# Residual and norm between the stages of a decoder layer: square sums chained on VectorE, weight casts queued behind the scaled rows, rounded rows written k-tile by k-tile

## The chip, the cores and the metric

One core of a Trainium2 chip runs the whole layer in one launch. The metric is device time in microseconds (us) of one execution; the number that counts is the median over several executions.

## The reference

One decoder layer, batch 1, 256 tokens, width 1024, in float32. Each of three sub-layers is normalised, modulated by a shift and a scale that come from a conditioning vector c, and added back under a gate:

```python
mod = (silu(c) @ w_ada + b_ada)                    # 9 vectors of 1024
sh1, sc1, gt1, sh2, sc2, gt2, sh3, sc3, gt3 = split(mod, 9)
n = rmsnorm(h, g_ffn1) * (1 + sc1) + sh1
h = h + 0.5 * gt1 * swiglu(n, w1_gate, w1_up, w1_down)      # d_ff = 2816
n = rmsnorm(h, g_mix) * (1 + sc2) + sh2
h = h + gt2 * hybrid_mixer(n, w_in, w_pool, pool_scale, w_out)
n = rmsnorm(h, g_ffn2) * (1 + sc3) + sh3
h = h + 0.5 * gt3 * swiglu(n, w2_gate, w2_up, w2_down)
return rmsnorm(h, g_final)
```

`rmsnorm(x, g)` is `x * rsqrt(mean(x*x) + 1e-6) * g`. The mixer projects n by `w_in` into four chunks of 512 columns (pool input u, then q, k, v), pools u over trailing windows, lets 8 heads attend over three dilated windows, and projects both by `w_out`.

## The kernel before

**Numbers.** Every large product is made of three matmuls. A float32 operand is split into a rounded part (`hi` for weights, `nh` for rows) and what is left (`lo`, `nl`); the matmuls are nh by hi, nl by hi and nh by lo, added up in PSUM (`gemm`, L344; `down`, L379; `lead_step`, L404). So each weight unit (128 x 2048 floats, 1 MB) that has landed in one of four `raw` buffers is cast twice per half: `hi` on ScalarE (L241) and `lo` on VectorE (L242), into one of 11 half-unit buffers each. The tokens are two tiles of 128 rows, t = 0 and t = 1.

**Order of the weights.** `plan()` writes out by hand the order of 114 units; SyncE's queue loads them in that order (L225) as `raw` buffers come free. Between the weight units stand 36 units called `ada`: two rows of `w_ada` per unit, multiplied by silu(c) and summed on VectorE (L230, two instructions for each unit), which gives two columns of `mod`. `want()` fetches so far ahead that five weight units lie behind the one in use. Around the first of the two norms that this change touches the order is: down 7, 8, 9, 10 of the first feed-forward with the last `ada` units that its norm needs; then `win` (1,0), ada, `win` (1,1), ada, `win` (2,0), ada, `win` (2,1), ada, `win` (3,0), ada, `win` (3,1). `win` (c, half) is half of the 1024 input rows of the projection's chunk c (1 is q, 2 is k, 3 is v, 0 is u). When `finish1(0)` is written, everything up to `win` (3,0) has been fetched, four `ada` units of the mixer's gate among it.

**Order on an engine.** The instructions of each engine are put in a fixed order when the program is built: a list schedule by priority, in which an instruction whose inputs are ready goes ahead of a more urgent one whose inputs are not. `urgent()` raises the priority of what stands on the path between stages, `ADA` lowers that of the `ada` products. On the chip each engine then runs its list in that order.

**First norm of the change (feed-forward 1 to mixer).** At the end of `ffn_rest` the held chunks 7 to 10 are multiplied for t = 0; `finish1(0)` adds the gated result to h (`residual`: one product and one sum for each 512 columns, VectorE), sums squares on ScalarE (`rstd`, L269), adds and raises to the power -0.5 on GpSimd (L271, L273, L275), and scales the rows on ScalarE (`norm_rows`, L294). Meanwhile TensorE multiplies the same four chunks for t = 1 (48 matmuls, L386). `after()` stands before chunk number `TURN` of them: it transposes the scaled rows of t = 0 (eight transposes, `turn`, L282), then `norm_mod` applies scale and shift and splits the result into nh and nl: columns 0 to 511 are scaled on ScalarE (L311), columns 512 to 1023 on VectorE (L313), each half is split by one cast and one subtraction of 512 columns (`split`, L260 and L261). Then `zchunk` (L345 to L347) runs q for t = 0 (q0, 24 matmuls), and k0. `finish1(1)` does the same for t = 1; its transposes stand inside k0, before k-tile 1. q1 follows, then k1, v0 and the rest.

**Second norm of the change (mixer to feed-forward 2).** `wout` runs t = 0, then t = 1 (48 matmuls, L675); `finish2(0)`'s transposes stand before its last chunk (`TURN1` = 3). The first four k-tiles of the second feed-forward (`lead_step`, L416) run for t = 0 alone; `finish2(1)`'s transposes stand before the last of them (`TURN2` = 3). Here columns 512 to 1023 are only copied (`xT3`, L304).

`rstd`, `norm_rows`, `norm_mod`, `residual`, `finish1`, `finish2`, `fetch` and the constants `TURN` and the new `AFTER1` are what the diff touches. Temporaries of 512 columns share three buffers (`t2`).

Of the kernel before, what the change touches and what calls it, by code (L numbers as in the profile page):

```python
# [15 lines left out]
P = 128  # L16
# [16 lines left out]
TURN = 2  # L33
TURN1 = 3
TURN2 = 3
T2 = 3
# [132 lines left out]
def block_kernel(ctx, tc, w, vec, x, c, gf, wpool, bandd, biasd, out):  # L169
# [46 lines left out]
    ready = {}  # L216
    done_mod = set()
    place = {u: i for i, u in enumerate(order)}

    def fetch():  # L220
# [5 lines left out]
        if kind == "ada":  # L226
            with tc.high_priority(offset=ADA if i >= 2 * KD else 0):
                for s, m in enumerate(a):
                    r = raw[:, ts(s, D)]
                    nc.vector.tensor_tensor_reduce(  # L230
                        r, r, cb, 1.0, vecs[:, m:m + 1], ALU.mult, ALU.add, mod[:, m:m + 1])
                    done_mod.add(m)
            return
        his, los = [], []
        for s in range(2):
# [3 lines left out]
            for o in range(0, 1024, n):  # L239
                src = raw[:, s * 1024 + o:s * 1024 + o + n]  # L240
                nc.scalar.copy(hi[:, o:o + n], src)  # L241
                nc.vector.tensor_tensor(lo[:, o:o + n], src, hi[:, o:o + n].bitcast(F32), ALU.subtract)  # L242
# [21 lines left out]
    def rstd(t, tag):  # L264

        ss = tiny.tile([P, 2], F32, name=f"ss{tag}", tag="ss")
        for b in range(2):
            sq = work.tile([P, 512], F32, name=f"sq{tag}{b}", tag="t2", bufs=T2)
            nc.scalar.activation(sq, h[:, t * D + b * 512:t * D + b * 512 + 512], AF.Square, accum_out=ss[:, b:b + 1])  # L269
            if b == 0:  # L270
                nc.gpsimd.tensor_tensor(ss[:, 0:1], ss[:, 0:1], deps, ALU.add)  # L271
        v = tiny.tile([P, 1], F32, name=f"v{tag}", tag="v")
        nc.gpsimd.tensor_tensor(v, ss[:, 0:1], ss[:, 1:2], ALU.add)  # L273
        r = tiny.tile([P, 1], F32, name=f"r{tag}", tag="r")
        nc.gpsimd.tensor_tensor(r, v, mhalf, ALU.pow)  # L275
        return r

# [11 lines left out]
    def norm_rows(t, tag):  # L289
        r = rstd(t, tag)  # L290
        xs = []
        for b in range(2):
            xs.append(work.tile([P, 512], F32, name=f"xs{tag}{b}", tag="t2", bufs=T2))
            nc.scalar.activation(xs[b], h[:, t * D + b * 512:t * D + b * 512 + 512], AF.Copy, scale=r)  # L294
        return xs

    def norm_mod(xs, which, shm, tag, t=None, xT=None):

        nh, nl = new_n(tag)
        for b in range(2):  # L300
            pt = turn(xs[b], f"xt{tag}{b}")
            with urgent():
# [4 lines left out]
                for i in range(4):  # L307
                    j = 4 * b + i
                    a, s = acol[:, which * KD + j:which * KD + j + 1], mod[:, shm * KD + j:shm * KD + j + 1]
                    if b == 0:  # L310
                        nc.scalar.activation(n32[:, i, :], pt[:, i, :], AF.Identity, bias=s, scale=a)  # L311
                    else:
                        nc.vector.tensor_scalar(n32[:, i, :], pt[:, i, :], a, s, ALU.mult, ALU.add)  # L313
# [464 lines left out]
```

## Time and profile before

| what | value |
|---|---|
| median of 3 runs | 495.44 us (495.12 to 497.16) |
| the profiled execution | 498.72 us, of which its span from the first to the last instruction is 496.7 us |
| busy: TensorE, VectorE, ScalarE, GpSimd | 476.4 us (96%), 355.3 us (72%), 257.6 us (52%), 17.2 us (3%) |
| mean granted TensorE clock | 0.995 |

Busy times are from one profiled execution; the span is what the trace covers. A share of 96% for TensorE says that it has little idle time, not where that lies.

### The profile page before, as it was taken

How to read it: one execution, taken by the hardware profiler on the slowest of the kernel's cores; microseconds unless marked ns; L12 is line 12 of the kernel's file. 1: busy time of each engine (PE TensorE's matmuls, PEld its weight loads, DVE VectorE, ACT ScalarE, POOL GpSimd, SP SyncE). 2: the span in 40 equal slices, each digit the busy share in tenths (PEclk: the TensorE clock that was granted, in tenths of full speed). 3: DMA queues.
4: the chain of work that ended last, by engine and by line, in shares of the span. 5: the costliest groups of instructions: out<-in, count | busy, mean ns of one | idle time of the engine just before them, and what ended most of it. 6: DMA issues, size and time to landing. Idle time of an engine off the chain costs nothing.

```text
span 496.7 us, 5926 instructions
## 1 busy us (share of the span) xinstructions
PE 476.4 (96%) x2151; PEld 383.6 (77%) x2151; DVE 355.3 (72%) x568; ACT 257.6 (52%) x435; POOL 17.2 (3%) x26
## 2 busy tenths in 40 slices
PE   4899999999999999899999999999999999999994
PEld 2688888888888888678766877888878888888883
DVE  5887979997797897698868767555656656655244
ACT  2667575453355453574777458945543443544121
POOL 1000000000000001120000022000000000000000
PEclk9999999999999999899999999999999999999999
DMA  8999975899988897769865847395266758540102
GB/s 318 354 336 356 346 292 201 326 364 406 338 323 330 332 328 273 266 244 379 349 226 193 284 155 281 102 367 177 105 242 252 277 221 329 185 164 2 42 2 84
DMA packets 20095, 126.05 MB, mean 254 GB/s; under 512 B 2377, under 2 KB 4193, under 8 KB 5474
## 3 DMA queue, kind: packets, MB, share of 16 engines
q1 hardware_dynamic: 17280, 121.25, 65.0%
q10 hardware_dynamic: 2786, 4.43, 2.7%
q8 instruction: 17, 0.28, 0.2%
q14 instruction: 12, 0.10, 0.0%
HBM read 124.61 MB, written 1.06 MB: 253 GB/s over the span
## 4 chain that ended last, share of the span: by engine, by line
PE 86%; ACT 3%; DVE 2%; DMA 2%; issue 2%; POOL 2%; POOLq 0%; ACTq 0%; DVEq 0%
PE accf L386 21%; PE ld L416 9%; PE le L416 9%; PE gu L345 9%; PE gu L347 9%; PE gu L346 9%; PE zp L345 3%; PE zp L347 3%; PE zp L346 3%; PE ht L372 2%; PE accm L675 1%; DMA gfb<-in_gf_dram 1%; ACT hi L241 1%; DMA vecs<-in_vec_dram 1%; PE sh L345 1%
## 5 line engine op out<-in xcount | busy, mean ns | idle before, releaser
L242 DVE TENSOR_TENSOR lo<-raw,hi 128x1024 fp32r<-128x1024 f32 (+1 forms) x160 | 186.8, 1195 | 49.7 <-ACT hi L241 41.3
L241 ACT CAST hi<-raw 128x1024 fp32r<-128x1024 f32 (+1 forms) x160 | 160.3, 1031 | 78.3 <-PE accf L386 24.9
L230 DVE CUSTOM_DVE_ANT_0 raw<-raw,cb,vecs 128x1024 f32<-128x1024 f32 x72 | 90.5, 1279 | 6.6 <-DMA raw<-in_w_dram 6.6
L386 PE MATMUL accf<-hi,hh 128*128 128x512 f32 x176 | 56.2, 395 | 0.2
L386 PE MATMUL accf<-lo,hh 128*128 128x512 f32 x176 | 56.3, 394 | 0.0
L386 PE MATMUL accf<-hi,hl 128*128 128x512 f32 x176 | 55.7, 390 | 0.0
L345 PE MATMUL gu<-hi,nhc 128*128 128x512 f32 x112 | 44.4, 397 | 0.0
L347 PE MATMUL gu<-lo,nhc 128*128 128x512 f32 x112 | 43.7, 390 | 0.0
L346 PE MATMUL gu<-hi,nlc 128*128 128x512 f32 x112 | 43.6, 390 | 0.0
L363 ACT ACTIVATE sg<-gu 128x256 f32<-128x256 f32 x24 | 9.2, 381 | 64.4 <-PE gu L347 61.7
L386 PEld LDWEIGHTS accf<-lo,hh 128*128 128x128 f32 x176 | 33.3, 189 | 6.9
L386 PEld LDWEIGHTS accf<-hi,hl 128*128 128x128 f32 x176 | 32.8, 188 | 7.4 <-DVE hl L261 0.7
L386 PEld LDWEIGHTS accf<-hi,hh 128*128 128x128 f32 x176 | 32.7, 190 | 7.4 <-ACT hh L260 1.1
L366 DVE TENSOR_TENSOR pr<-sg,gu 128x256 f32<-128x256 f32 x24 | 10.1, 419 | 32.2 <-ACT sg L363 32.2
L345 PE MATMUL gu<-hi,nha 128*128 128x512 f32 x80 | 31.8, 397 | 0.0
L346 PE MATMUL gu<-hi,nla 128*128 128x512 f32 x80 | 31.2, 390 | 0.0
L347 PE MATMUL gu<-lo,nha 128*128 128x512 f32 x80 | 31.2, 390 | 0.0
L345 PE MATMUL zp<-hi,nhb 128*128 128x512 f32 x64 | 26.7, 417 | 0.0
L347 PE MATMUL zp<-lo,nhb 128*128 128x512 f32 x64 | 25.3, 395 | 0.0
L346 PE MATMUL zp<-hi,nlb 128*128 128x512 f32 x64 | 25.2, 394 | 0.0
L347 PEld LDWEIGHTS gu<-lo,nhc 128*128 128x128 f32 x112 | 21.0, 188 | 4.5
L345 PEld LDWEIGHTS gu<-hi,nhc 128*128 128x128 f32 x112 | 21.0, 188 | 4.3
(162 smaller groups left out, 694.6 us busy)
## 6 DMA issues: line engine op xcount, KB each, us to landing
raw<-in_w_dram SPq DMA_DIRECT2D x114, 1024.0 KB, 5.4
gt<-gd ACTq DMA_DIRECT2D x3, 512.0 KB, 5.0
h<-in_x_dram SPq DMA_DIRECT2D x2, 512.0 KB, 4.7
bias<-in_bias_dram ACTq DMA_DIRECT2D x4, 256.0 KB, 4.4
out_dram<-o SPq DMA_DIRECT2D x4, 160.0 KB, 2.1
bands<-in_band_dram ACTq DMA_DIRECT2D x4, 136.0 KB, 2.4
gfb<-in_gf_dram ACTq DMA_DIRECT2D x1, 512.0 KB, 5.9
out_dram<-o ACTq DMA_DIRECT2D x2, 192.0 KB, 2.1
```

What stands on the lines that cost most here:

```text
L230: nc.vector.tensor_tensor_reduce(r, r, cb, 1.0, vecs[:, m:m + 1], ALU.mult, ALU.add, mod[:, m:m + 1])
L241: nc.scalar.copy(hi[:, o:o + n], src)
L242: nc.vector.tensor_tensor(lo[:, o:o + n], src, hi[:, o:o + n].bitcast(F32), ALU.subtract)
L345: mm(ps, nh[:, k, :], whi, start=first, stop=False)
L346: mm(ps, nl[:, k, :], whi, start=False, stop=False)
L347: mm(ps, nh[:, k, :], wlo, start=False, stop=last)
L363: nc.scalar.activation(sg, ps[:, 0:256], AF.Silu)
L366: nc.vector.tensor_tensor(pr, sg, ps[:, 256:512], ALU.mult)
L372: nc.tensor.transpose(pt[:, i, :], pr[:, ts(i, P)], ident)
L386: mm(accs[b], a[:, k, :], cols(ww, 2 * k + b), start=st, stop=sp)
L416: mm(banks[ci][t], n[t][a][:, j, :], cols(ww, lead_set(f, j).index(ci)), start=j == 0 and p == 0, stop=last and p == 2)
L675: mm(acc2[t][b], a[:, k, :], cols(ww, 2 * kk + b), start=st, stop=sp)
```

## The change

- The square sums of a row go from ScalarE (with two additions on GpSimd) to VectorE: one multiply-and-sum instruction for each 512 columns, the second one starting from the first one's result, the first from D times EPS. They stand right behind the residual, in the same function. GpSimd keeps the power alone.
- Of the two scaled halves of a row tile, the second is made on VectorE.
- `casts_after` adds, on ScalarE's and on VectorE's list, an order: weight casts from a given half unit on, and `ada` products from a given unit on, stand behind the scaled rows. For t = 0 of the first norm these are the casts from the second half of `win` (1,1) on, for t = 1 those from `win` (2,1) on, and both times the `ada` products from the unit behind `win` (1,0) on. For the second norm: casts from the second half of lead 1 on (t = 0) and from lead 3 on (t = 1), `ada` from lead 2 on.
- `norm_mod` writes the rounded part of each k-tile straight from PSUM on ScalarE, the unrounded k-tile and the rest on VectorE, k-tile by k-tile (128 columns).
- The transposes of t = 0 stand one chunk later (`TURN` 2 to 3), those of t = 1 two k-tiles later in k0 (`AFTER1` = 3, was 1), those of q0's heads at k-tile 5, was 3.

```diff
@@ -30,9 +30,10 @@
 HOLD = 4
 AHEAD = 5
 URGENT = 400
-TURN = 2
+TURN = 3
 TURN1 = 3
 TURN2 = 3
+AFTER1 = 3
 T2 = 3
 WOUT = (2, 0, 1, 3)
 ADA = -60
@@ -214,8 +215,32 @@
 
     pos = [0]
     ready = {}
+    bulk = []
+    queues = {}
     done_mod = set()
     place = {u: i for i, u in enumerate(order)}
+
+    def order_dep(late, early, reason):
+        tc.add_manual_dep(late, early.name, mybir.DependencyInfo(
+            mybir.DependencyClass.NoSync, mybir.DependencyReason.DATA), reason=reason)
+
+    def behind(cast, unit, kind):
+
+        units, first = queues.get(cast.ins.engine, ((1e9, 1e9), None))
+        if unit >= units[kind]:
+            order_dep(cast.ins, first, "casts later")
+
+    def casts_after(firsts, units):
+
+        for f in firsts:
+            queues[f.engine] = (units, f)
+        for cast in bulk:
+            if any(cast[0].ins.engine == f.engine for f in firsts):
+                behind(*cast)
+
+    def note(cast, unit, kind):
+        bulk.append((cast, unit, kind))
+        behind(cast, unit, kind)
 
     def fetch():
         i = pos[0]
@@ -227,8 +252,8 @@
             with tc.high_priority(offset=ADA if i >= 2 * KD else 0):
                 for s, m in enumerate(a):
                     r = raw[:, ts(s, D)]
-                    nc.vector.tensor_tensor_reduce(
-                        r, r, cb, 1.0, vecs[:, m:m + 1], ALU.mult, ALU.add, mod[:, m:m + 1])
+                    note(nc.vector.tensor_tensor_reduce(
+                        r, r, cb, 1.0, vecs[:, m:m + 1], ALU.mult, ALU.add, mod[:, m:m + 1]), i, 1)
                     done_mod.add(m)
             return
         his, los = [], []
@@ -238,8 +263,8 @@
             n = 1024 // (2 if i in (1, 2 * KD - 1) else 1)
             for o in range(0, 1024, n):
                 src = raw[:, s * 1024 + o:s * 1024 + o + n]
-                nc.scalar.copy(hi[:, o:o + n], src)
-                nc.vector.tensor_tensor(lo[:, o:o + n], src, hi[:, o:o + n].bitcast(F32), ALU.subtract)
+                note(nc.scalar.copy(hi[:, o:o + n], src), i + s / 2, 0)
+                note(nc.vector.tensor_tensor(lo[:, o:o + n], src, hi[:, o:o + n].bitcast(F32), ALU.subtract), i + s / 2, 0)
             his.append(hi)
             los.append(lo)
         ready[(kind, a)] = (his, los)
@@ -261,20 +286,6 @@
         nc.vector.tensor_tensor(lo_ap, src, hi_ap.bitcast(F32), ALU.subtract)
 
 
-    def rstd(t, tag):
-
-        ss = tiny.tile([P, 2], F32, name=f"ss{tag}", tag="ss")
-        for b in range(2):
-            sq = work.tile([P, 512], F32, name=f"sq{tag}{b}", tag="t2", bufs=T2)
-            nc.scalar.activation(sq, h[:, t * D + b * 512:t * D + b * 512 + 512], AF.Square, accum_out=ss[:, b:b + 1])
-            if b == 0:
-                nc.gpsimd.tensor_tensor(ss[:, 0:1], ss[:, 0:1], deps, ALU.add)
-        v = tiny.tile([P, 1], F32, name=f"v{tag}", tag="v")
-        nc.gpsimd.tensor_tensor(v, ss[:, 0:1], ss[:, 1:2], ALU.add)
-        r = tiny.tile([P, 1], F32, name=f"r{tag}", tag="r")
-        nc.gpsimd.tensor_tensor(r, v, mhalf, ALU.pow)
-        return r
-
     def turn(src, name):
 
         pt = psp.tile([P, 4, P], F32, name=name, tag="ps")
@@ -286,12 +297,23 @@
         return (npool.tile([P, KD, P], F32R, name=f"nh{tag}", tag="nh"),
                 npool.tile([P, KD, P], F32R, name=f"nl{tag}", tag="nl"))
 
-    def norm_rows(t, tag):
-        r = rstd(t, tag)
-        xs = []
+    def norm_rows(t, tag, accs, g, units):
+
+        ss = None
         for b in range(2):
-            xs.append(work.tile([P, 512], F32, name=f"xs{tag}{b}", tag="t2", bufs=T2))
-            nc.scalar.activation(xs[b], h[:, t * D + b * 512:t * D + b * 512 + 512], AF.Copy, scale=r)
+            tmp = work.tile([P, 512], F32, name=f"res{tag}{b}", tag="t2", bufs=T2)
+            nc.vector.tensor_tensor(tmp, accs[b], g[:, ts(b, 512)], ALU.mult)
+            hs = h[:, t * D + b * 512:t * D + b * 512 + 512]
+            nc.vector.tensor_tensor(hs, hs, tmp, ALU.add)
+            v = tiny.tile([P, 1], F32, name=f"v{tag}{b}", tag="v")
+            nc.vector.tensor_tensor_reduce(tmp, hs, hs, 1.0, D * EPS if ss is None else ss, ALU.mult, ALU.add, v)
+            ss = v
+        r = tiny.tile([P, 1], F32, name=f"r{tag}", tag="r")
+        nc.gpsimd.tensor_tensor(r, ss, mhalf, ALU.pow)
+        xs = [work.tile([P, 512], F32, name=f"xs{tag}{b}", tag="t2", bufs=T2) for b in range(2)]
+        rows = [nc.scalar.activation(xs[0], h[:, t * D:t * D + 512], AF.Copy, scale=r),
+                nc.vector.tensor_scalar(xs[1], h[:, t * D + 512:t * D + D], r, None, ALU.mult)]
+        casts_after([i.ins for i in rows], units)
         return xs
 
     def norm_mod(xs, which, shm, tag, t=None, xT=None):
@@ -307,11 +329,9 @@
                 for i in range(4):
                     j = 4 * b + i
                     a, s = acol[:, which * KD + j:which * KD + j + 1], mod[:, shm * KD + j:shm * KD + j + 1]
-                    if b == 0:
-                        nc.scalar.activation(n32[:, i, :], pt[:, i, :], AF.Identity, bias=s, scale=a)
-                    else:
-                        nc.vector.tensor_scalar(n32[:, i, :], pt[:, i, :], a, s, ALU.mult, ALU.add)
-                split(nh[:, 4 * b:4 * b + 4, :], nl[:, 4 * b:4 * b + 4, :], n32)
+                    nc.scalar.activation(nh[:, j, :], pt[:, i, :], AF.Identity, bias=s, scale=a)
+                    nc.vector.tensor_scalar(n32[:, i, :], pt[:, i, :], a, s, ALU.mult, ALU.add)
+                    nc.vector.tensor_tensor(nl[:, j, :], n32[:, i, :], nh[:, j, :].bitcast(F32), ALU.subtract)
         return nh, nl
 
     def scale_cols(which, scm, lo=0, hi=KD):
@@ -332,13 +352,6 @@
         g = work.tile([P, D], F32, name=f"gt{gtm}", tag="gt", bufs=1)
         nc.scalar.dma_start(g, d.rearrange("(o a) b -> o (a b)", o=1).to_broadcast([P, D]))
         return g
-
-    def residual(t, accs, g, tag):
-        for b in range(2):
-            tmp = work.tile([P, 512], F32, name=f"res{tag}{t}{b}", tag="t2", bufs=T2)
-            nc.vector.tensor_tensor(tmp, accs[b], g[:, ts(b, 512)], ALU.mult)
-            hs = h[:, t * D + b * 512:t * D + b * 512 + 512]
-            nc.vector.tensor_tensor(hs, hs, tmp, ALU.add)
 
 
     def gemm(ps, nh, nl, k, whi, wlo, first, last):
@@ -519,8 +532,8 @@
         with urgent():
             if t == 0:
                 scale_cols(1, SC2)
-            residual(t, nm["acc"][t], nm["g"], "a")
-            xs = norm_rows(t, f"b{t}")
+            xs = norm_rows(t, f"b{t}", nm["acc"][t], nm["g"],
+                           (place["win", (1, 1)] + 0.5 if t == 0 else place["win", (2, 1)], place["win", (1, 0)]))
         return lambda: nm.update({t: norm_mod(xs, 1, SH2, f"b{t}")})
 
     prs[2] = [second_half(2, t) for t in range(NT)]
@@ -641,7 +654,7 @@
         return go
 
     z["q0"] = zchunk(1, 0, QS)
-    z["k0"] = zchunk(2, 0, 1.0, {1: after, 3: turn_heads("q0", qT, 0)})
+    z["k0"] = zchunk(2, 0, 1.0, {AFTER1: after, 5: turn_heads("q0", qT, 0)})
     z["q1"] = zchunk(1, 1, QS, {3: turn_heads("k0", kT, 0)})
     z["k1"] = zchunk(2, 1, 1.0, {3: turn_heads("q1", qT, 1)})
     sc = [lambda hd=hd: scores(hd) for hd in range(HEADS)]
@@ -680,8 +693,9 @@
         with urgent():
             if t == 0:
                 scale_cols(2, SC3, 0, KD // 2)
-            residual(t, acc2[t], nm["g2"], "m")
-            xs = norm_rows(t, f"c{t}")
+            xs = norm_rows(t, f"c{t}", acc2[t], nm["g2"],
+                           (place["lead", (1, 1)] + 0.5, place["lead", (1, 2)]) if t == 0 else
+                           (place["lead", (1, 3)], place["lead", (1, 2)]))
         return lambda: n3.update({t: norm_mod(xs, 2, SH3, f"c{t}", t, xT3)})
 
     wout(0, (0, 1))
```

## Rows read from the trace of the kernel before

**Rows 1.** The page's parts 1 and 4: busy time, and the chain that ended last.
```profile
PE 476.4 (96%) x2151; PEld 383.6 (77%) x2151; DVE 355.3 (72%) x568; ACT 257.6 (52%) x435; POOL 17.2 (3%) x26
...
PE 86%; ACT 3%; DVE 2%; DMA 2%; issue 2%; POOL 2%; POOLq 0%; ACTq 0%; DVEq 0%
```

**Rows 2.** The chain in order of time: start us, us, what.
```profile
124.92 5.44 PE accf L386 x24
...
199.43 1.43 POOL rb L275
200.88 0.73 ACT xsb L294
...
214.91 0.73 ACT xsb L294
```

**Rows 3.** Timeline of TensorE, 184 to 222 us: start, length, what, [idle before <- releaser].
```profile
192.70 0.62 PE L386 MATMUL accf<-lo,hh 128*128 128x512 f32 x2
...
198.60 0.61 PE L386 MATMUL accf<-hi,hl 128*128 128x512 f32 x2
201.66 1.12 PE L282 MATMUL xtb<-ident,xsb 128*128 128x128 f32 x4 [2.44 <-ACT xsb L294]
...
208.53 0.39 PE L345 MATMUL zp<-hi,nhb 128*128 128x512 f32 x1
...
215.68 1.27 PE L282 MATMUL xtb<-ident,xsb 128*128 128x128 f32 x8 [0.87 <-ACT xsb L294]
```

**Rows 4.** Busy time by stretch; after the five engines the granted clock, DMA share, GB/s.
```profile
201.66:204.28 2.62, 2.62 (x10) 2.35 (x11) 0.13 (x1) 1.97 (x6) 0.00 (x0) 0.50 0.84 341
...
214.80:215.68 0.88, 0.02 (x1) 0.00 (x0) 0.88 (x3) 0.77 (x2) 0.07 (x1) 1.00 0.66 251
```

**Rows 5.** Timeline of TensorE around the second norm, 268 to 318 us.
```profile
297.55 1.27 PE L282 MATMUL xtc<-ident,xsc 128*128 128x128 f32 x8 [0.23 <-ACT xsc L294]
...
302.43 1.19 PE L416 MATMUL le<-hi,nhc 128*128 128x512 f32 x4 [0.86 <-ACT nhc L260]
```

**Rows 6.** Timeline of VectorE, 184 to 222 us.
```profile
192.13 1.28 DVE L230 CUSTOM_DVE_ANT_0 raw<-raw,cb,vecs 128x1024 f32<-128x1024 f32 x1
...
193.34 1.28 DVE L339 TENSOR_TENSOR resa<-accf,gt 128x512 f32<-128x512 f32 x2
...
204.15 1.37 DVE L313 TENSOR_SCALAR n32b<-xtb,acol,mod 128x128 f32<-128x128 f32 x4 [3.71 <-issue]
...
210.92 2.35 DVE L242 TENSOR_TENSOR lo<-raw,hi 128x1024 fp32r<-128x1024 f32 x2
```

**Rows 7.** Timeline of all engines at the last norm, 482.8 to 484.4 us.
```profile
483.27 0.55 POOL L731 TENSOR_TENSOR ro<-vo,mhalf 128x1 f32<-128x1 f32 x1 [1.35 <-DVE vo L729]
...
483.85 0.68 DVE L733 TENSOR_SCALAR o<-o,ro 128x320 f32<-128x320 f32 x2 [0.66 <-POOL ro L731]
```

**Rows 8.** VectorE's groups by form: xcount | busy us, mean ns | idle before.
```profile
L242 DVE TENSOR_TENSOR lo<-raw,hi 128x1024 fp32r<-128x1024 f32 x152 | 181.7, 1222 | 49.7 <-ACT hi L241 41.3 <-PE le L416 6.2
L230 DVE CUSTOM_DVE_ANT_0 raw<-raw,cb,vecs 128x1024 f32<-128x1024 f32 x72 | 90.5, 1279 | 6.6 <-DMA raw<-in_w_dram 6.6
...
L261 DVE TENSOR_TENSOR nlb<-n32b,nhb 128x512 fp32r<-128x512 f32 x4 | 2.6, 688 | 1.0 <-ACT nhb L260 1.0
...
L402 DVE TENSOR_TENSOR nlc<-n32l,nhc 128x128 fp32r<-128x128 f32 x8 | 2.0, 289 | 1.3 <-ACT n32l L400 1.3
...
L470 DVE TENSOR_SCALAR xs<-h,rx 128x1024 f32<-128x1024 f32 x2 | 1.5, 751 | 0.4 <-POOL rx L468 0.4
...
L733 DVE TENSOR_SCALAR o<-o,ro 128x320 f32<-128x320 f32 x4 | 1.4, 384 | 1.3 <-POOL ro L731 1.3
```

**Rows 9.** Timeline of SyncE's queue: the load of `win` (2,1).
```profile
193.45 0.33 SPq L225 DMA_DIRECT2D raw<-in_w_dram  x1
```

**Rows 10.** The loads' line, 170 to 260 us: time from issue to landing.
```profile
DMA to landing us min/median/max: 4.7/5.0/9.5
```

**Rows 11.** ScalarE's groups by form, 193 to 222 us.
```profile
L241 ACT CAST hi<-raw 128x1024 fp32r<-128x1024 f32 x8 | 8.5, 1056 | 3.6 <-PE accf L386 3.6
```

## The prediction, made before the result was known

> **What bounds the kernel now.** I read the page first: TensorE is busy 96% of the span and makes 86% of the chain that ended last; VectorE is busy 72% [rows 1]. So a microsecond that TensorE waits is a microsecond of the result, and work on the other engines counts only where TensorE waits for it. Then I followed the chain in order of time. It is matmuls, 24 of 512 columns in 5.44 us or 0.227 us each, except where it crosses over at the norms: GpSimd's power, then ScalarE's scaled row, then the transposes [rows 2]. TensorE's timeline there shows four waits [rows 3, 5]. Before the transposes of the first norm, t = 0, it idles 2.44 us; for t = 1, 0.87 us; in the second norm 0.23 us before the transposes of t = 0 and 0.86 us before the first matmul that uses them, which waited for ScalarE's cast of nh. The first wait has a second price: in the 2.62 us right behind it the granted clock is 0.50, the lower level of 1.2 GHz, though TensorE is busy throughout; behind the 0.87 us it stays at 1.00 [rows 4]. At full clock that stretch would have taken half, 1.31 us less. These five figures, 2.44 + 1.31 + 0.87 + 0.23 + 0.86 = 5.71 us, are all that the change can take away here.
>
> **Part 1, the later transposes (TURN, AFTER1).** The transposes of t = 0 now stand where TensorE stood at 198.60 us plus some eight more matmuls (three chunks are 36; the schedule had already put two pairs past the second one), so TensorE comes to them at 199.2 + 1.8 = 201.0 us instead of standing still from 199.2. Even the old chain, whose first row was done at 200.88 + 0.73 = 201.6 us [rows 2], would then cost only 0.6. Nothing is lost by it unless q0, which uses these rows, comes too early: q0 would begin at 208.53 - 2.44 - 1.31 = 204.8 us, 3 us behind the transposes' end. For t = 1 TensorE comes to the transposes 33 matmuls after that: 204.8 + 7.5 = 212.3 us.
>
> **Part 2, the chain of residual, squares and rows.** VectorE began the residual at 193.34 us, when an `ada` product that had started at 192.13 was through [rows 6]; this product is now queued behind the rows, and the last matmul pair for t = 0 began at 192.70 and ran 0.62 us [rows 3], so 193.2 is a fair start. Two 512-column instructions take 1.28 us at a mean of 0.68, a step of 0.60 [rows 6]. The new multiply-and-sum has no row at 512 columns here; the bounds are 0.60 (that step) and 0.75 (the 1024-column one's 1.28 less 0.53, by which a subtraction of 1024 columns, 1.222, is longer than one of 512, 0.688 [rows 8]); I take 0.65. Four steps and two sums: 4 x 0.60 + 2 x 0.65 = 3.7, so 196.9 us. Then the power. In the old chain it took 1.43 us [rows 2]. With VectorE idle, as the last norm has it, it took 0.55 [rows 7]. For t = 0 every cast and product that could run beside it is now behind the rows, so I take 0.55, with 1.43 as the other bound. ScalarE's row takes 0.73 [rows 2]; VectorE's half lies between the 0.384 of 320 columns and the 0.751 of 1024 [rows 8], about 0.48. Rows of t = 0 are ready at 198.3 (199.2 by the other bound), against TensorE's 201.0: the 2.44 us and the 1.31 us behind it go, with a cover of 1.8 to 2.7 us.
>
> The Trainium skill has a rule on that power ("SBUF — State Buffer", section "Who interferes with whom"): GpSimd shares a pair of SBUF ports with VectorE, and one of the two holds it for a whole instruction. By it the 0.9 us between the two rows are waiting, and a power behind which casts are deferred takes the short time; without it the sum would take 1.43 for both. The trace's two lengths agree with it; that no other cause makes the long one, no row shows.
>
> **Part 3, k-tile by k-tile.** VectorE's scaling steps from PSUM are 1.37 us for four at a mean of 0.40, a step of 0.32 [rows 6], and a subtraction of 128 columns is 0.289 long against 0.688 for 512 [rows 8]; at a step of 0.2 to 0.25 a k-tile costs VectorE 0.52 to 0.57 us. A k-tile feeds three matmuls, 0.68 us, so the stream keeps ahead of TensorE once it has begun. But all eight k-tiles of a tile now cost VectorE 4.2 to 4.6 us, where it had 1.4 + 2 x 0.69 = 2.8. ScalarE loses four scalings, a square pair and the second row and is no limit. In the second norm this takes away the 0.86 us: the first matmul needs k-tile 0 alone, and no longer four scalings and a cast in a row behind two weight casts.
>
> The Trainium skill speaks against this part ("Perfetto Trace Analysis", section "Optimizing Scalar/DVE Operations"): every instruction pays a fixed overhead, and larger ones are better where the engine is saturated, smaller ones where it only makes others wait. The lengths of 128 and 512 columns above agree. By the first half of that rule the pieces cost 1.5 us for each tile, by the second they are free; which half holds is the first rival.
>
> **Part 4, what is queued behind the rows.** After the rows of t = 0 three half units (`win` (1,1) second half, `win` (2,0)) stand at the head: hi 1.06 us each on ScalarE [rows 11], lo 1.22 on VectorE [rows 8]. The first lo can run at about 199.5. Between 199.5 and TensorE's 212.3 VectorE has three lo casts (3.6), the k-tiles (4.4) and the chain of t = 1 (3.7, not before 204.8), then power and row (1.3 to 2.2). If one cast goes ahead of the k-tiles, the k-tiles end at 205.7, the rows of t = 1 are there at 210.7 to 211.6, and there is no wait; if all three do, at 208 and at 213 to 214, a wait of 0.7 to 1.7. I take 0.4. Both rows together: the old 0.87 becomes 0.4.
>
> The four `ada` units stay in their `raw` buffers until the rows of t = 1, since the order is renewed for t = 1 from the same unit on. There are four buffers. `win` (2,1) was loaded at 193.45 [rows 9], the moment the product that ran from 192.13 to 193.41 freed a buffer [rows 6]; that buffer now stays full. The next one goes to a further `ada` unit, so `win` (2,1) waits for the casts of `win` (2,0): 203 us if they run ahead of the k-tiles, 212 if behind. A load lands 5.0 us after its issue [rows 10]. Its own casts are behind the rows of t = 1 too, at 211 to 214, plus 1.06 and 1.22: ready at 213.3 to 216.3 us, while k0 asks for it at 212.3 + 1.0 + 0.7 = 214. What hides it: the list can put q1's matmuls, which need the rows of t = 1 only, in front. Cost 0 to 2.3, I take 0.4. `win` (3,0) and (3,1) come later by the same buffers. The lo casts of `win` (2,1), which free one, ran at 210.92 before [rows 6]; now they end at 216 to 221, and with an `ada` unit loaded first `win` (3,0) lands some 7.5 us on, at 224 to 229. v0 uses it 96 matmuls and their transposes after q0's start, at about 229; I take 0.3, between 0 and 2.
>
> In the second norm the same deferral has a 1 us longer cover (TensorE comes at 297.3, and the row was 0.23 late by the old chain), so I count no new wait.
>
> **The sum.** 5.71 - 0.4 - 0.4 - 0.3 = 4.6 us less. The profiled execution took 498.72 us, 3.3 above the median; from it the sum gives 494.1. The terms are waits between engines that each execution has, so I take the same 4.6 from the median: 490.8 us. This case: 489.3 (nothing comes back) to 492.6.
>
> **Rivals.** (1) *VectorE becomes the bound at the first norm.* All three casts go ahead, the power of t = 1 is long, and TensorE waits some 2.4 us at the transposes of t = 1, enough to fall to the lower clock again as it did after 2.44: 5.71 - 2.4 - 1.31 = 2.0 less, 493.4. For it: VectorE was idle 3.71 us in the old stretch [rows 6] and gains 1.3 + 0.5 + 1.5 us of work for each tile. Against: lo casts that no one needs yet can give way. (2) *The buffers.* `win` (2,1) is loaded only after the casts behind the chain of t = 1, at 212 to 213, lands at 217 to 218 and is cast by 220: TensorE, at 214, waits 6 us, drops its clock (1.31), and the next units come 1 us late. 5.71 - 0.4 - 6 - 1.31 - 1 = -3.0, so 498.4. It decides once the load is issued after about 211. For it: three of four buffers are held by units that may not run. Against: matmuls of q1 fill the hole. (3) *It doesn't do what it says:* the waits move to the next point where rows are used (q0, q1, the leads), or a row is late by the same power, and at most 1 us is won: 495.
>
> **Chances.** The forecast 0.55, rival 1 0.2, rival 2 0.13, rival 3 0.12. A measurement of this kernel tells 0.5%, 2.5 us, from no change: 492.96 and 497.92 are the bounds. Faster: 0.55, and two fifths of rival 1, 0.63. Slower: rival 2, 0.13. The same: 0.24. For eight in ten the range goes from 489.0 (all 5.71 and a few tenths for transposes at full clock) through rivals 1 and 3 to 495.6.
>
> **What would show it.** Right: no idle before the transposes of t = 0 and a clock of 1.00 behind them; a power of about 0.55 for t = 0; q0 at some 204.8 us; the first lead matmul without a wait; the load of `win` (2,1) at 203 to 212. Wrong: idle of over 1.5 us before the transposes of t = 1 with VectorE full (rival 1), matmuls of k0 or q1 waiting for casts whose load came late (rival 2), or new waits at q0 (rival 3). What would upset all of it is a different order on VectorE than the one I assume, above all casts inside a chain.

## The result, and the profile after

The changed kernel took 493.41 us (median of 13 executions, 492.79 to 494.59). The kernel before, in turns with it on the same chip, took 496.46 us (13 executions, 494.54 to 498.84). The ratio is 0.9945, with a 95% interval of 0.9928 to 0.9962: by it 2.7 us were gained (the medians differ by 3.05), of the 4.6 forecast. The forecast time, 490.8, was 2.6 us too low; the measured one lies inside the stated range of 489.0 to 495.6. Two executions on record, of 1681 us (the kernel before) and 2705 us (`halves_act`, below), stand in no median or ratio here.

The profiled execution of the changed kernel took 493.41 us itself, span 491.6. Beside the 498.72 of the one before that would be 5.3 us, so one of these two executions does not stand for its median. The page's busy times and the shares of the chain by engine, against [rows 1]:

```profile
PE 474.8 (97%) x2151; PEld 382.0 (78%) x2151; DVE 367.9 (75%) x622; ACT 250.9 (51%) x417; POOL 6.3 (1%) x18
...
PE 85%; DVE 8%; issue 2%; ACT 2%; DMA 1%; POOL 1%; POOLq 0%; ACTq 0%; DVEq 0%
```

VectorE has 12.6 us more work, ScalarE 6.7 and GpSimd 10.9 less. TensorE's waits, the view that lists who waited for whom (total us, times, longest), of the changed kernel:

```profile
PE ld L429 <- ACT hi L266: 3.3, 1, 3.3
PE xt L293 <- DVE xs L483: 2.7, 1, 2.7
PE pc L466 <- DMA crow<-in_c_dram: 2.4, 1, 2.4
PE zp L360 <- DVE lo L267: 0.5, 1, 0.5
PE zp L359 <- DVE nlb L334: 0.2, 1, 0.2
```

The first three belong to the kernel's start and are as before. No wait stands at a norm's transposes (`xtb`, `xtc`) or at the leads (`le`). TensorE's timeline shows the same, against [rows 3]; the last row is a stretch by windows, whose third figure from the end is the granted clock, against [rows 4]:

```profile
200.32 1.03 PE L293 MATMUL xtb<-ident,xsb 128*128 128x128 f32 x8
...
203.96 0.39 PE L358 MATMUL zp<-hi,nhb 128*128 128x512 f32 x1
...
206.80 0.50 PE L359 MATMUL zp<-hi,nlb 128*128 128x512 f32 x1 [0.19 <-DVE nlb L334]
...
214.54 0.71 PE L358 MATMUL zp<-hi,nhb 128*128 128x512 f32 x2
215.74 0.50 PE L360 MATMUL zp<-lo,nhb 128*128 128x512 f32 x1 [0.48 <-DVE lo L267]
```

```profile
190.00:230.00 40.00, 39.32 (x185) 31.60 (x185) 35.10 (x74) 18.60 (x32) 1.10 (x2) 1.00 0.57 205
```

All five terms of the prediction's sum are absent from this profile, q0 begins at 203.96 us (forecast 204.8), the clock stays at 1.00, and what came in their place is 0.19 and 0.48 us. VectorE's timeline of the first norm, against [rows 6]:

```profile
192.58 1.29 DVE L305 TENSOR_TENSOR resb<-accf,gt 128x512 f32<-128x512 f32 x2 [2.12 <-PE accf L399]
193.79 1.28 DVE L307 TENSOR_TENSOR h<-h,resb 128x512 f32<-128x512 f32 x2
194.99 0.69 DVE L309 CUSTOM_DVE_ANT_0 resb<-h 128x512 f32<-128x512 f32 x1
...
195.72 0.75 DVE L309 CUSTOM_DVE_ANT_0 resb<-h,vb 128x512 f32<-128x512 f32 x1
...
197.21 0.48 DVE L315 TENSOR_SCALAR xsb<-h,rb 128x512 f32<-128x512 f32 x1 [0.73 <-POOL rb L312]
198.91 3.50 DVE L267 TENSOR_TENSOR lo<-raw,hi 128x1024 fp32r<-128x1024 f32 x3 [1.21 <-ACT hi L266]
...
211.33 0.49 DVE L315 TENSOR_SCALAR xsb<-h,rb 128x512 f32<-128x512 f32 x1 [0.73 <-POOL rb L312]
211.73 1.28 DVE L255 CUSTOM_DVE_ANT_0 raw<-raw,cb,vecs 128x1024 f32<-128x1024 f32 x1
...
214.46 1.22 DVE L267 TENSOR_TENSOR lo<-raw,hi 128x1024 fp32r<-128x1024 f32 x1
```

The chain runs as drawn: residual, two sums, power, rows of t = 0 at 197.2 to 197.9 us (forecast 198.3, old 201.6). All three deferred `lo` casts then go ahead of the k-tiles, which the prediction had left open. The rows of t = 1 come at 211.3 to 211.8, two `ada` products follow, and only then the `lo` of `win` (2,1) at 214.46, for which TensorE waits 0.48 us.

### The profile page after: what moved, and what is told of

Its sections match the earlier page's. It is cut to its first block, busy times and chain, and to the rows that moved or that the text cites. A ratio compares the mean times of both kernels' runs of the same rounds, so it can differ in the third digit from the quotient of the medians.

```text
span 491.6 us, 5927 instructions
## 1 busy us (share of the span) xinstructions
PE 474.8 (97%) x2151; PEld 382.0 (78%) x2151; DVE 367.9 (75%) x622; ACT 250.9 (51%) x417; POOL 6.3 (1%) x18
## 4 chain that ended last, share of the span: by engine, by line
PE 85%; DVE 8%; issue 2%; ACT 2%; DMA 1%; POOL 1%; POOLq 0%; ACTq 0%; DVEq 0%
PE accf L399 20%; PE ld L429 9%; PE gu L358 9%; PE gu L360 9%; PE gu L359 9%; PE le L429 7%; PE accm L688 4%; PE zp L360 3%; PE zp L358 3%; PE zp L359 2%; PE ht L385 2%; DVE lo L267 1%; DVE raw L255 1%; DMA vecs<-in_vec_dram 1%; PE yt L616 1%
## 5 line engine op out<-in xcount | busy, mean ns | idle before, releaser
L286 DVE TENSOR_TENSOR hl<-ht,hh 128x256 fp32r<-128x256 f32 x44 | 16.4, 417 | 11.0 <-ACT hh L285 11.0
```

Source lines behind the costliest of these rows:

```text
L286: nc.vector.tensor_tensor(lo_ap, src, hi_ap.bitcast(F32), ALU.subtract)
```

## Experiments

Two theories of the missing 1.9 us (4.6 less 2.7). **A:** of the five terms, some belong to the one execution that was profiled and not to the median. **B:** the change gives time back later: the pieces of 128 columns, the buffers or the deferral cost more than was allowed.

### The kernel before, twice more

Unchanged, for theory A.

> The kernel before, unchanged, profiled once more. Theory 1: the profiled execution of before was one of its slower ones (498.72 us against a median of 496.46), and the 2.44 us of idle or the 1.31 us of low clock before and behind the first transposes are not in each execution; then this profile, if it is of a faster execution, shows a shorter idle or a clock of 1.00 there, and the executions lie in groups about 1.3 us apart. Theory 2: each execution pays both, and before's executions differ elsewhere (the start, the loads); then this profile shows 2.3 to 2.6 us of idle and the clock at 0.50 for about 3 us again, whatever its time. Ratio 1.000 either way.

> A third profile of the kernel before. Theory 1 (its profiled execution was one of several kinds): 2.4 to 2.5 us of idle before the transposes of t = 0 and 0.87 before those of t = 1 in each; the clock behind the first at 0.50 in some and at 1.00 in others; the 0.23 and 0.86 us of the second norm in some only. Theory 2 (all alike): clock 0.50 for 3 us and all four waits.

495.73 us, ratio 0.9985 (0.9963 to 1.0007), and 494.9 us for the single execution of before_look. Both profiles show the same: waits of 2.47 and 0.86 or 0.87 us at the first norm, no clock drop there, none of the second norm's waits. In before_again: TensorE at the first norm, the clock around it (by windows), and GpSimd's power for t = 0 of the second norm:

```profile
201.52 0.66 PE L282 MATMUL xtb<-ident,xsb 128*128 128x128 f32 x4 [2.47 <-ACT xsb L294]
```

```profile
200.00:204.30 4.30, 2.78 (x16) 2.45 (x17) 1.66 (x6) 3.36 (x7) 0.71 (x1) 1.00 0.89 322
```

```profile
293.11 0.55 POOL L275 TENSOR_TENSOR rc<-vc,mhalf 128x1 f32<-128x1 f32 x1
```

The same idle time, 2.47 us, is followed by a clock of 1.00, not of 0.50. The power took 0.55 us, where the execution behind [rows 5] had 1.49, and the second norm's 0.23 and 0.86 us are absent. What differs beside the power is the start of a `lo` cast on VectorE. Here are the power and the cast in the execution behind [rows 5], then the cast in before_again:

```profile
295.24 1.49 POOL L275 TENSOR_TENSOR rc<-vc,mhalf 128x1 f32<-128x1 f32 x1
```

```profile
295.10 1.23 DVE L242 TENSOR_TENSOR lo<-raw,hi 128x1024 fp32r<-128x1024 f32 x1 [0.26 <-ACT hi L241]
```

```profile
293.18 1.23 DVE L242 TENSOR_TENSOR lo<-raw,hi 128x1024 fp32r<-128x1024 f32 x1 [0.47 <-ACT hi L241]
```

The long power began 0.14 us behind a cast, the short one 0.07 us ahead of it. All 72 powers of these two norms in the 18 profiles of this document fall so: 27 began 0.14 to 0.23 us behind a `lo` cast or an `ada` product and took 1.40 to 1.50 us, 45 began with no such instruction running and took 0.55. So, of the prediction's five terms, three, 1.31 + 0.23 + 0.86 = 2.40 us, are not in these two; 2.47 + 0.87 = 3.34 are in all three. The mean granted clock of every execution is a hint of how often the first happens: of 84 of the kernel before in four comparisons, 27 had 0.994 or less and took 497.58 us in the median, 53 had 0.996 or more and took 495.60 (four lay between). Of 19 of the changed kernel none was under 0.995, and their 493.4 is 2.2 us less than 495.60. Theory A holds: the profiled execution was a dear one. The 0.5 us between 2.2 and the measured 2.7 are about what the slower group adds to the mean of the kernel before. That the drop at the first norm makes this group is inferred, not shown: only three executions of the kernel before were profiled, the one with the drop has 0.995, between the groups, and the clock falls in the last norm too (from 475 to 495 us it is 0.84 in the changed kernel, 0.90 in before_again).

### Part 1 alone

```diff
-TURN = 2
+TURN = 3
```

> The kernel before with the transposes of t = 0 one chunk later (TURN = 3) and nothing else. The rows were ready at 201.6 us, TensorE comes at 201.0: 0.6 us of idle are left and no low clock, 3.1 us less in the profile up to there. Theory A (the later place alone is the gain): q0 begins 3 us earlier and the time falls by 2.5 to 3.1 us. Theory B (without the faster split the gain moves on): q0 comes 3.6 us after the transposes, the old split with its 512-column casts took some 4 to 5 us, so q0 waits 0.6 to 1.5 us; time falls by 1.5 to 2.5 us.

496.79 us, ratio 1.0002 (0.9982 to 1.0022). TensorE's waits in it:

```profile
PE xtb L282 <- ACT xsb L294: 2.1, 2, 1.4
PE le L416 <- ACT nhc L260: 1.4, 1, 1.4
PE zp L346 <- DVE nlb L261: 0.5, 1, 0.5
PE zp L345 <- ACT nhb L260: 0.5, 1, 0.5
```

At t = 0 TensorE now waits 0.6 us, as the prediction had it for the old chain, but it waits twice 0.5 at q0, 1.4 at t = 1 and 1.4 at the leads: the third rival's mechanism. With the other two places moved as well:

```diff
-    z["k0"] = zchunk(2, 0, 1.0, {1: after, 3: turn_heads("q0", qT, 0)})
+    z["k0"] = zchunk(2, 0, 1.0, {3: after, 5: turn_heads("q0", qT, 0)})
```

> As the last, and the transposes of t = 1 two k-tiles later too (AFTER1 = 3). The rows of t = 1 came 0.87 us after TensorE; now TensorE comes 1.36 us later, so this idle goes. Theory A: 0.9 us less than with TURN = 3 alone, 3.4 to 4 us less than before, and the new chain brings nothing more. Theory B: the stages behind absorb it, as the profile of after has q0 to the end of the projections no shorter than before (62.8 against 62.7 us): the same as TURN = 3 alone within 0.5 us.

495.72 us, 0.9984 (0.9961 to 1.0006): the wait at t = 1 falls to 0.3 us, those at q0 and the leads stay. And the other way round, all of the change but the places:

```diff
-TURN = 3
+TURN = 2
...
-    z["k0"] = zchunk(2, 0, 1.0, {AFTER1: after, 5: turn_heads("q0", qT, 0)})
+    z["k0"] = zchunk(2, 0, 1.0, {1: after, 3: turn_heads("q0", qT, 0)})
```

> The changed kernel with both transposes at their old places (TURN = 2, AFTER1 = 1), so the new chain, the deferral and the split alone. TensorE comes to the transposes of t = 0 some 26 matmuls or 5.9 us after the last matmul of t = 0; the new rows take 5.3 us in the profile of after (192.6 to 197.9). Theory A (the places are the gain): 1 us or less of idle before each and the time within 1 us of the changed kernel's or 1 us above. Theory B (the chain is the gain): no idle for t = 0, the same time as the changed kernel within 0.5 us. For t = 1 the rows come 6.9 us after the last matmul, TensorE after 6.1: 0.8 us of idle by both.

492.80 us, 0.9915 (0.9883 to 0.9947). The places bring nothing alone, and with the pieces of 128 columns nothing is lost without them (with halves it is otherwise, see halves_early below): with the new chain the rows are nearly there in time for the old places. The transposes of t = 0 wait 0.2 us; the 0.8 us of idle expected at t = 1 did not come, but TensorE waited 0.8 us for a `hi` cast of the projection.

### The queue behind the rows

```diff
-        casts_after([i.ins for i in rows], units)
```

> The changed kernel without the order that puts casts and ada products behind the rows. Theory A (the deferral carries the gain): casts and products of 1.2 us stand inside the chains and beside the power, which then takes 1.4 us instead of 0.55; rows of t = 0 come 1 to 3 us later than 197.9, those of t = 1 too; TensorE, which comes at 200.3 and 212.1, idles 0.5 to 2 us at one of them or at both and the time rises 1 to 3 us over the changed kernel. Theory B (the chain and the later places have cover enough): within 0.7 us of the changed kernel.

493.90 us, 0.9957 (0.9941 to 0.9973). GpSimd's power for t = 0:

```profile
199.59 1.40 POOL L312 TENSOR_TENSOR rb<-vb,mhalf 128x1 f32<-128x1 f32 x1 [189.18 <-DVE vb L309]
```

Without the order the power takes 1.40 us in place of 0.55, close to the prediction's other bound of 1.43, but TensorE waits only 0.5 us at t = 1 and 0.4 at the leads. The time, 0.9957 against 0.9945, is not told from the changed kernel's: the intervals overlap. Half the order is worse than none (`ada` products deferred for t = 0 only, casts for both):

```diff
-                           (place["win", (1, 1)] + 0.5 if t == 0 else place["win", (2, 1)], place["win", (1, 0)]))
+                           (place["win", (1, 1)] + 0.5 if t == 0 else place["win", (2, 1)], place["win", (1, 0)] if t == 0 else 1e9))
...
-                           (place["lead", (1, 3)], place["lead", (1, 2)]))
+                           (place["lead", (1, 3)], 1e9))
```

> The changed kernel with the ada products behind the rows of t = 0 alone and no longer behind those of t = 1 (both norms); weight casts as changed. Theory A (buffers held by ada units cost time): win (2,1) is loaded before 202.4 us, the 0.48 us of waiting in k0 go, and the units behind it come 5 us or more earlier: 0.5 us faster than the changed kernel. Theory B (VectorE is the bound): products of 1.2 us each stand in the chain of t = 1, whose rows came 0.1 us before TensorE needed them: idle of 1.2 to 2.5 us there and the power at 1.4 us: 1 to 3 us slower than the changed kernel.

495.53 us, 0.9992 (0.9978 to 1.0007): the whole gain is lost. The power of t = 1 ran beside the products, and TensorE waited 2.35 us for the row (and 1.0 us at a row of the second norm):

```profile
213.11 1.46 POOL L312 TENSOR_TENSOR rb<-vb,mhalf 128x1 f32<-128x1 f32 x1 [15.64 <-DVE vb L309]
```

```profile
215.38 1.09 PE L293 MATMUL xtb<-ident,xsb 128*128 128x128 f32 x8 [2.35 <-ACT xsb L314]
```

### Square sums back on ScalarE

```diff
-            nc.vector.tensor_tensor_reduce(tmp, hs, hs, 1.0, D * EPS if ss is None else ss, ALU.mult, ALU.add, v)
-            ss = v
+            nc.scalar.activation(tmp, hs, AF.Square, accum_out=ss[:, b:b + 1])
+            if b == 0:
+                nc.gpsimd.tensor_tensor(ss[:, 0:1], ss[:, 0:1], deps, ALU.add)
...
+        nc.gpsimd.tensor_tensor(v, ss[:, 0:1], ss[:, 1:2], ALU.add)
```

> The changed kernel with the squares on ScalarE and the two additions on GpSimd again; deferral, split, second half row on VectorE and places as changed. Theory A (squares on VectorE matter): two squares 1.3, three GpSimd instructions of 0.2 to 0.55 with VectorE quiet, 1.3 in all, against 1.35 and 0.55: rows about 0.7 us later. t = 0 has 2.4 us of cover at 200.3, so nothing there; t = 1 has 0.1 and idles 0.6: 0.5 to 0.8 us over the changed kernel. Theory B (VectorE is the bound at t = 1): 1.3 us less work on VectorE before the rows of t = 1, no idle there, the same or up to 0.5 us faster.

493.02 us, 0.9946 (0.9919 to 0.9972), as the changed kernel: no gain of the squares' move is seen, as long as casts stay behind the rows. The twelve executions lie between 491.37 and 497.90 us, so a difference under a microsecond would not show.

### Halves in place of the pieces

`norm_mod` as before the change (four scalings, one cast, one subtraction of 512 columns); all else changed.

```diff
-                    nc.scalar.activation(nh[:, j, :], pt[:, i, :], AF.Identity, bias=s, scale=a)
-                    nc.vector.tensor_scalar(n32[:, i, :], pt[:, i, :], a, s, ALU.mult, ALU.add)
-                    nc.vector.tensor_tensor(nl[:, j, :], n32[:, i, :], nh[:, j, :].bitcast(F32), ALU.subtract)
+                    if b == 0:
+                        nc.scalar.activation(n32[:, i, :], pt[:, i, :], AF.Identity, bias=s, scale=a)
+                    else:
+                        nc.vector.tensor_scalar(n32[:, i, :], pt[:, i, :], a, s, ALU.mult, ALU.add)
+                split(nh[:, 4 * b:4 * b + 4, :], nl[:, 4 * b:4 * b + 4, :], n32)
```

> The changed kernel with the old split of the rounded rows: scaling of columns 0 to 511 on ScalarE, 512 to 1023 on VectorE, one cast and one subtraction for each 512 columns. Theory A (the k-tiles carry the gain): as in the kernel with TURN = 3 alone, q0 waits 0.5 twice and the first lead matmul 1.35 us: 2 to 2.5 us over the changed kernel. Theory B (only the time from the last matmul to the rows matters): at most 0.7 us over it.

490.76 us, 0.9903 (0.9878 to 0.9927), beating both kernels, which neither theory had. Two combinations were meant to add to it:

> The kernel with the old split (halves) and the old places of the transposes (TURN = 2, AFTER1 = 1) as well: what is left of the change is the chain, the second half row and the deferral. Theory A (the two findings add up: the pieces cost 2 us, the later places bring nothing): 0.990 of before or less, within 0.5 us of halves. Theory B (the old split needs the later place, since it is slower from transposes to the last half): q0 waits 0.5 to 1 us or t = 1 idles 0.8, 1 us or more above halves.

> The kernel with the old split and the squares on ScalarE again; deferral, second half row on VectorE and later places as changed. VectorE has 1.6 us less work for each tile by the split and 1.3 by the squares. Theory A (VectorE's load from the rows on is what the changed kernel pays): as fast as halves or up to 1 us faster, 0.988 to 0.990 of before. Theory B (with the split in halves VectorE is not the bound any more, and the squares' way over two engines and three GpSimd instructions only makes the rows later): 0 to 1 us slower than halves.

> The changed kernel unchanged, beside the kernels of this group on one chip. Theory: 0.9945 of before again (0.993 to 0.996), its profile with no idle before any transposes and the clock at 1.00, as it has cover where before had none; the executions spread by 2 us, before's by 4.

On one chip these came out at 493.29 (0.9947, 0.9927 to 0.9966), 492.77 (0.9942, 0.9923 to 0.9962) and, for the changed kernel again, 493.43 (0.9950, 0.9933 to 0.9966). The gain was gone in both; for halves_act that lies outside both theories. Their longest new waits are of other kinds, TensorE for `nhb` and for a cast of z, here in halves_early and then in halves_act:

```profile
PE zp L360 <- ACT nhb L285: 1.0, 1, 1.0
```

```profile
PE tk L293 <- ACT z L575: 1.8, 1, 1.8
```

Was the gain of halves an accident, then? Four more runs, one after the other on one chip:

> The kernel of the run halves once more, on another chip. If the pieces really cost some 2 us, the ratio to the kernel before comes near 0.990 again (measured there: 0.9903, after 0.9945 and 0.9950). If that gain was an accident of one chip, it comes out at 0.994 to 0.995.

> Pieces written k-tile by k-tile in the second norm only; in the first norm again four scalings and one cast of 512 columns. In the profile of halves the gain lies at the two stages behind the first norm, z (1.3 us) and the output projection (1.0 us). If VectorE's load at the first norm is the price of the pieces, this has nearly all of the gain: ratio 0.990 to 0.991, the next two win units loaded some 4 us earlier than after.

> Pieces in the first norm only; in the second norm again halves. If the price lies at the first norm, this is as after: 0.994 to 0.995. The second norm then loses what the pieces bring there: a wait of up to 0.9 us at the first lead matmul, as before had, so 0.994 to 0.996. If the price lies at the second norm, it is 0.990 to 0.991.

> The kernel of halves without the order that keeps weight casts behind the rows. With that order undone the kernel after lost 0.1 per cent at most (0.9957 against 0.9945). If halves are worth 2 us by themselves, this is at 0.991; if they only pay together with the queueing, at 0.994 to 0.996, and the power of the first norm is 1.4 us long again.

| kernel | median, us | ratio to before (95%) |
|---|---|---|
| halves_again | 491.02 | 0.9880 (0.9852 to 0.9908) |
| halves_first (halves at the first norm only) | 492.40 | 0.9906 (0.9879 to 0.9933) |
| halves_second (halves at the second norm only) | 493.31 | 0.9931 (0.9906 to 0.9956) |
| halves_no_queue | 493.84 | 0.9947 (0.9926 to 0.9968) |

It repeats, and it needs the queue: by the ratios the order is worth 3.3 us with halves (2.2 from the first run's 0.9903), and 0.6 with pieces, which the intervals do not tell from nothing. By the medians halves at the first norm alone bring 1.0 us against the changed kernel's 493.41, at the second alone 0.1, at both 2.4, so the two parts do not add up; the greater part that one norm alone brings is the first's. VectorE's timeline in halves shows why the pieces are not free:

```profile
198.47 3.49 DVE L267 TENSOR_TENSOR lo<-raw,hi 128x1024 fp32r<-128x1024 f32 x3 [1.21 <-ACT hi L266]
201.88 1.36 DVE L335 TENSOR_SCALAR n32b<-xtb,acol,mod 128x128 f32<-128x128 f32 x4
...
208.97 0.48 DVE L315 TENSOR_SCALAR xsb<-h,rb 128x512 f32<-128x512 f32 x1 [0.73 <-POOL rb L312]
...
211.79 1.22 DVE L267 TENSOR_TENSOR lo<-raw,hi 128x1024 fp32r<-128x1024 f32 x1
```

From the end of the three casts to the second row of t = 1 it takes 208.97 - 201.88 = 7.1 us with hardly a gap; in the changed kernel 211.33 - 202.32 = 9.0. The 1.9 us are the pieces' (forecast 1.5). Every cast behind the second row is 1.9 us and more later for it, and so is the next load of a `win` unit by SyncE, here in the changed kernel and then in halves:

```profile
220.22 0.33 SPq L250 DMA_DIRECT2D raw<-in_w_dram  x1
```

```profile
215.45 0.33 SPq L250 DMA_DIRECT2D raw<-in_w_dram  x1
```

From q0 (203.96 and 203.51 us) to the first lead matmul (296.87 and 294.08) the changed kernel takes 92.9 us, halves 90.6. TensorE's timeline of the changed kernel, of halves and of before_again:

```profile
296.87 1.07 PE L429 MATMUL le<-hi,nhc 128*128 128x512 f32 x4
```

```profile
203.51 0.39 PE L360 MATMUL zp<-hi,nhb 128*128 128x512 f32 x1
...
294.08 1.07 PE L431 MATMUL le<-hi,nhc 128*128 128x512 f32 x4
```

```profile
207.02 0.39 PE L345 MATMUL zp<-hi,nhb 128*128 128x512 f32 x1
...
299.37 1.19 PE L416 MATMUL le<-hi,nhc 128*128 128x512 f32 x4
```

Only 0.67 of the 2.3 us are waits. The rest carries no mark of a wait. Nor is all of it a loss against the kernel before: that takes 92.35 us here, 91.5 without its wait of 0.87, the changed kernel 92.2 without its own, halves 90.6. So some 0.8 us is what the changed kernel lost, and 0.9 is what halves gain beyond the kernel before, a gain that no forecast had.

The rest is read here as the order of the same 441 matmuls: the list schedule, given later casts, turns from the projections to the small matmuls of the attention and back more often (71 changes from one target tile to another on TensorE's timeline against 64). TensorE's timeline of the output projection, in the changed kernel and in halves:

```profile
278.15 0.65 PE L616 MATMUL yt<-pts,z 128*64 128x256 f32 x2
278.63 0.38 PE L617 MATMUL yt<-pts,z 128*64 128x128 f32 x2
278.94 0.50 PE L688 MATMUL accm<-hi,nhy 128*128 128x512 f32 x1
...
280.76 0.65 PE L616 MATMUL yt<-pts,z 128*64 128x256 f32 x2
281.24 0.38 PE L617 MATMUL yt<-pts,z 128*64 128x128 f32 x2
281.55 0.73 PE L688 MATMUL accm<-hi,nly 128*128 128x512 f32 x2
```

```profile
276.13 0.66 PE L618 MATMUL yt<-pts,z 128*64 128x256 f32 x4
276.61 0.40 PE L619 MATMUL yt<-pts,z 128*64 128x128 f32 x4
276.93 0.50 PE L690 MATMUL accm<-hi,nhy 128*128 128x512 f32 x1
```

Eight of them in one visit take 276.93 - 276.13 = 0.80 us; in two visits of four, 278.94 - 278.15 = 0.79 and again 0.79. No idle time is marked, so no view of waits shows this 0.8 us. One visit is not enough, though. Another eight of the changed kernel, whose two lines alternate, take 246.76 - 245.59 = 1.17 us, and halves have such a visit too:

```profile
245.59 0.81 PE L616 MATMUL yt<-pts,z 128*64 128x256 f32 x3
...
246.76 0.49 PE L359 MATMUL zp<-hi,nlb 128*128 128x512 f32 x1
```

What halves_early and halves_act lost is another matter, mostly marked waits: 1.5 and 2.4 us in sum, behind casts that their own order put late. The count of changes is no measure by itself, though: no_queue has 66 and takes 93.3 us, the kernel before has 63 and takes longer than halves, and act_squares, with the pieces and 67 changes, takes 90.6 in its profile, as halves do. So the pieces alone do not make the stretch long; act_squares has 1.3 us less of squares on VectorE for each tile. No run fixed the order by hand: that the order makes the rest was read from the timelines, not tested.

## Why the prediction was off

**The step that failed** is the last one of the sum: "The terms are waits between engines that each execution has, so I take the same 4.6 from the median: 490.8 us." The profiled execution lay 3.3 us above the median, which the prediction noted and then let go by. Of its 5.71 us, 2.40 (the 1.31 behind the first wait, the 0.23 and the 0.86) were in that execution and in neither of two others. Without them the same working gives 3.3 - 1.1 = 2.2 us from the median, 493.2, against 493.41 measured. From the profiled execution's own time it gave 494.1, and the profiled execution after took 493.41.

**Luck in that agreement.** The 1.1 us that the prediction gave back came back in other places. Set beside before_again (span 493.7 us, against 491.6), the changed kernel has waits of 0.67 instead of 3.34 us. It gains 3.1 us up to q0, where the wait was 2.47, and loses 0.8 in the unmarked part of the stretch from q0 to the first lead matmul and 0.4 behind it (194.7 against 194.3 us to the end). No wait came at the transposes of t = 1 (0.4 taken) and none at v0 (0.3 taken). Luck too is that the first rival named 493.4 us: its wait of 2.4 us and its second clock drop did not happen. The forecast's lower bound, 489.3 for "nothing comes back", is not its own sum: 495.44 - 5.71 = 489.7.

**The first norm** (parts 1 and 2) went as worked out: rows at 197.2 us, power 0.55, q0 at 203.96, no idle time at the transposes. That the power's length goes with VectorE's work beside it, the rule of the Trainium skill ("SBUF — State Buffer", section "Who interferes with whom"), the runs bear out: 0.55 for all four in the changed kernel, 1.40 without the order, 1.46 beside `ada` products. More closely, it goes with an instruction of VectorE that has begun before the power (above). But its weight was over-rated: in the changed kernel without the order the later transposes cover it at t = 0, and 0.5 us is left at t = 1. Part 1 alone took the wait at t = 0 down to 0.6 us, as worked out, and brought nothing: of "Nothing is lost by it unless q0, which uses these rows, comes too early" the condition came true, at q0 and behind it.

**The pieces** (part 3) were priced about right, 1.9 us of VectorE against 1.5, and taken to be hidden. They are not against halves: 2.1 us by the ratios (0.9945 against 0.9903), with no wait at the transposes of t = 1. That is the first rival in a mild form. But by the profiles only some 0.8 us of unmarked time and the 0.67 of new waits are a loss against the kernel before; what carries the unmarked part is open. The first half of the other rule of the Trainium skill, "Perfetto Trace Analysis", section "Optimizing Scalar/DVE Operations", agrees with this: VectorE is busy 35.10 of the 40 us from 190 to 230. The share alone does not tell pieces from halves, which have 35.15 there. At the second norm halves_second does not tell pieces from halves.

**The buffers** (part 4, second rival): `win` (2,1) was loaded at 202.43 us instead of 193.45, forecast for 203 to 212, and its `lo` came late for TensorE, which waited 0.48 us (0.4 taken). Two matmuls that do not need it stand before that wait (214.54 us), as the list was expected to put some; whether they are q1's the view does not say. That later casts also change the order of the matmuls, above, was not foreseen.

## What to carry to other kernels

Before a sum of waits is taken from a median, ask whether the profiled execution stands at that median; where it lies above, some of its waits and clock drops are its own, and a second profile says which. Split an engine's work into small pieces only where someone waits for the first piece and the engine has room: here the pieces cost VectorE 1.9 us for a tile at a load of 88%. In a kernel whose order a list schedule makes, an edit that delays casts also reorders the matmuls, and edits that each gain need not add up.

## What was not expected of the hardware

The granted clock after nearly the same idle time was not the same: 0.50 behind 2.44 us, 1.00 behind 2.47 in two other executions, and 1.00 behind 2.35 in ada_once. What decides it no run here shows. Eight small attention matmuls took 0.80 us in one visit of TensorE and 1.17 in another, four took 0.79. In the short visit of eight, four of 256 columns in a row take 0.66 us, as long as two (0.65), which points to two heads that run side by side; no run tested it.

A power of 128 x 1 on GpSimd took 0.55 us or 1.40 to 1.50, by whether a cast or product of VectorE had begun 0.14 to 0.23 us before it; one that began 0.07 us behind the power left it at 0.55.
